# Two products instead of three for small experts, with a branch that only TensorE takes, in a one-core MoE layer

## The chip, the cores and the metric

The kernel runs on one core of a Trainium2 chip. The metric is the device time of one execution in microseconds (us). Five engines work side by side, each with an instruction queue that it executes in order: PE (TensorE, matrix products; PEld is its weight load), DVE (VectorE), ACT (ScalarE), POOL (GpSimd, here mostly indirect DMAs) and SP (which issues the weight loads). They wait for one another through semaphores.

## What is computed

One trunk layer over 1024 tokens of width 1024: a token mixer, and then a hierarchical mixture of experts. The change touches the experts alone. Cut to them, the reference is

```python
g_idx = argmax(hf @ router_w_group + b)            # 1 of 4 groups
top_p, top_i = top_k(softmax(expert logits of that group), 2)
e_idx = g_idx * 8 + top_i                          # 2 of 32 experts for each token
...
hid = silu(x_e @ w_gate[e]) * (x_e @ w_up[e])      # x_e: the tokens of expert e, width 1024; FF = 512
y_e = hid @ w_down[e]                              # back to width 1024
out[token] += weight[token, e] * y_e
```

All in float32. With these inputs the reference's routing gives 21 experts at most 64 tokens, 6 experts 65 to 128, and 5 experts more than 128 (140, 143, 169, 193 and 194).

## The kernel before

The kernel runs the mixer, then the routing, and then a loop over the 32 experts that is fully unrolled in Python (L1823 to L1881), in the order `seq`. An expert's tokens are gathered into blocks of 128 slots (rows that no token fills are padding). The five experts with more than 128 tokens have a second block, called over.

Float32 accuracy comes from splitting both operands of a product in a high and a low part that TensorE multiplies at full rate: `split` (L90) writes high with ACT and low = source - high with DVE, and `mm3` (L94) makes high*high, high*low and low*high. The weights of an expert are six granules of 1 MB, loaded by SP into a ring of eight buffers (`raw`), and `spl(e, i)` splits granule i of expert e in two halves: two ACT instructions (`hi`, 128x1024) and two DVE instructions (`lo`, 128x1024). Granules 0 and 1 are gate and up of the first half of the width, 2 and 3 of the second half, 4 and 5 the down projection.

One iteration of the loop, for expert e, does in the order of the code:

- `part(e, 1, o, ...)` for gate (o = 0) and up (o = 1): the second half of the width, 4 times `mm3` each, 128x512 products that add in the PSUM banks `g` and `u`. Between the two, `xhalf` transposes the first half of the next expert's tokens (4 transposes, then `split` into `xh`, `xl`).
- If expert e has a second block (`tc.If` in L1831), the same for it. All engines take this branch.
- `act`: silu of bank `g` on ACT, times bank `u` on DVE, in `sg`.
- `part(e + 1, 0, 0, ...)`: gate of the next expert's first half. Then `hsplit`: four transposes of `sg`, and `split` into `hh`, `hl`.
- `xhalf` of the next expert's second half, `part(e + 1, 0, 1, ...)`, the branch of L1851 for second blocks, and `down(e, ...)`: 8 times `mm3` into the banks `y`.
- `emit`: two DVE instructions weigh `y` into `yt`, and POOL scatters `yt` to DRAM.

The `spl` calls for the following expert stand between these steps, and their places set the order of the `hi` on ACT and of the `lo` on DVE. Nothing is reordered at run time.

Of the kernel before, what the change touches and what calls it, by code (L numbers as in the profile page):

```python
# [20 lines left out]
P = 128  # L21
T = 1024
# [12 lines left out]
NB = 8  # L35
BIG = 128.0
HUGE = 1e30

# [11 lines left out]
def block_kernel(ctx: ExitStack, tc: tile.TileContext, I, out):  # L50
# [1201 lines left out]
    def pick(pl, i):  # L1252
        rr = sb(pl, "rr", [P, 2, 6, NE], BF16, bufs=3)
        return rr, V.tensor_tensor(rr, k2[:, i].unsqueeze(2).to_broadcast([P, 2, 6, NE]),
                                   vals[:, i].unsqueeze(3).to_broadcast([P, 2, 6, NE]), op=ALU.mult)
# [3 lines left out]
    def place(pl, i, b0, rr, ps):  # L1259
        oa = sb(pl, "oa", [P, 2, 2 * P], BF16, bufs=3)  # L1260
# [16 lines left out]
    def decode(pl, ps, out, ints):  # L1277
        us = []
        for b in range(2):
            v = ps[b].rearrange("p (f e) -> p f e", f=6)  # L1280
            u = sb(pl, f"u{b}", [P, 6, NE], bufs=1) if pl else sb(gt, "sgm", [P, 6, NE])
            us.append(u)
            V.tensor_copy(u[:, 0:2], v[:, 0:2])
            V.scalar_tensor_tensor(u[:, 0], u[:, 1], float(P), u[:, 0], op0=ALU.mult, op1=ALU.add)
            for dst in (out, ints)[::-1] if ints is not None else (out,):
                V.tensor_scalar(dst[:, b, :, 0], u[:, 0], -1.0, None, op0=ALU.add)
            yield
        for b, u in enumerate(us):
# [377 lines left out]
    def piece(e, i, k, n):  # L1666
        z, w = n * k // D, n * k % D
        return tuple(t_[:, w:w + n] for t_ in SP[e, i, z])

    def xhalf(xg, q, nm="x"):  # L1670
        x = q if nm == "x" else 0
        xh, xl = sb(wk, f"{nm}h{x}", [P, 4, P], F32R), sb(wk, f"{nm}l{x}", [P, 4, P], F32R)
# [45 lines left out]
    def over(e, q, banks):  # L1718
        if q == 0:
            warm(banks[0], 1.3)  # L1720
        xs = xhalf(xos[e % 2], q, "o")
        for o in range(2):
            part(e, q, o, xs, banks[o])

    full = xgs[0][:, 0:NB * NE * 3].rearrange("p (b e f) -> p b e f", b=NB, e=NE)

    def more(e, wf, banks, banks2):
# [6 lines left out]

        def tr(src, nm, n):
            o = sb(wk, nm, [P, 4, P])
            pt = sb(psm, "tp", [P, 4, P], bufs=2)
# [5 lines left out]
        for q in range(2):  # L1743
            xt = tr(xos[0], "xf", q)
# [4 lines left out]
        ht = tr(act(banks, "so"), "xf", 0)  # L1749
        for k in range(4):  # L1750
# [4 lines left out]

    NBV = {}

# [8 lines left out]
    def load_nb(e):  # L1766
        return nc.values_load(nbi[0:1, seq[e]:seq[e] + 1] if type(e) is int else e[0:1, :], min_val=0, max_val=NB)

    GU = [[sb(psm, f"{x}{i}", [P, FF]) for x in "gu"] for i in range(2)]
    ybank = [sb(psm, f"y{n}", [P, 512]) for n in range(2)]  # L1770
# [4 lines left out]
    for e in range(1, NX):  # L1775
        G.memset(xgs[e], 0.0)
        gather(xgs[e], e, 0)
    for o in range(2):
        part(0, 0, o, XA, GU[0][o])
    for x in xos:  # L1780
# [17 lines left out]
    def overflow(wf):  # L1798
        tp = [GU[1][0][:, b * 192:(b + 1) * 192] for b in range(2)]
        for b0 in range(2, NB, 2):  # L1800
            for i in range(NT):
                rr, _ = pick(wk, i)
                for _ in place(wk, i, b0, rr, tp):
                    pass
            for _ in decode(wk, tp, full[:, b0:b0 + 2], None):
                pass
# [16 lines left out]
    for e in range(NE):  # L1823
        nxt = e + 1 < NE
        A, B = GU[e % 2], GU[(e + 1) % 2]
        part(e, 1, 0, XB, A[0])
        if nxt:
            XA = xhalf(xgs[(e + 1) % NX], 0)
        part(e, 1, 1, XB, A[1])
        spl(e + 1, 1)  # L1830
        with tc.If(get_nb(e) > 1):  # L1831
            over(e, 1, B)
            sgo = act(B, "so")
        if not nxt:
# [25 lines left out]
        if not nxt:  # L1860
# [156 lines left out]
```

## Time and profile before

| | |
|---|---|
| median of 3 runs (lowest, highest) | 1670.95 us (1669.13, 1671.73) |
| profiled execution: its own time, its span | 1674.46 us, 1672.6 us |
| granted TensorE clock, mean over the span | 0.984 |
| busy: PE, DVE, ACT, POOL | 94%, 79%, 43%, 20% |
| loop over the experts | from about 890 to 1616 us of the span |

The span runs from the first to the last instruction of the profiled execution. Busy shares are averages over stages with different limits, so the loop has to be read by itself.

### The profile page before, as it was taken

The numbers are of one execution on the slowest core, as the hardware profiler recorded it, in microseconds if no ns is written. First come the engines' busy times: TensorE is split into PE (matmuls) and PEld (weight loads), VectorE is DVE, ScalarE is ACT, GpSimd is POOL, SyncE is SP. The second block draws the span as 40 slices with busy tenths as digits, with TensorE's granted clock in tenths as the row PEclk, the third lists the DMA queues.
The fourth block names the chain that finished last, engine by engine and source line by source line (L and its number), as shares of the span: only waits on it lengthen the run. The fifth ranks groups of instructions, "written<-read, shape, count | busy, mean of one in ns | idle before, by whom it ended". The sixth has DMA issues, their size and how long they took to land.

```text
span 1672.6 us, 23420 instructions
## 1 busy us (share of the span) xinstructions
PE 1570.5 (94%) x7602; PEld 1237.4 (74%) x7602; DVE 1320.1 (79%) x2917; ACT 725.3 (43%) x1053; POOL 330.5 (20%) x264
## 2 busy tenths in 40 slices
PE   7899999899998899999988999999999999999984
PEld 3688888778886777788866777777777777777751
DVE  7858883569998568878876786999986999686877
ACT  1533332341213342231122664777764777465622
POOL 1431000002234300003213121221221212120127
PEclk9999999999998999999989999999999999999998
DMA  8425788742314665656524695999995999676872
GB/s 320 163 76 167 230 244 263 239 166 98 100 60 131 167 179 164 202 194 229 184 77 162 251 340 191 348 364 363 362 345 182 361 356 377 259 284 240 290 296 101
DMA packets 141731, 381.61 MB, mean 228 GB/s; under 512 B 17632, under 2 KB 76160, under 8 KB 116992
## 3 DMA queue, kind: packets, MB, share of 16 engines
q1 hardware_dynamic: 130912, 362.80, 62.2%
q0 software_dynamic: 10656, 16.80, 2.7%
q8 instruction: 83, 1.36, 0.3%
q14 instruction: 80, 0.66, 0.1%
HBM read 336.98 MB, written 68.76 MB: 243 GB/s over the span
## 4 chain that ended last, share of the span: by engine, by line
PE 34%; DMA 24%; issue 21%; DVE 17%; POOL 1%; SPq 1%; POOLq 1%; another core or an unknown queue 0%; ACT 0%; DVEq 0%; ACTq 0%
DMA y_d<-yt,tbi 13%; DMA xo<-h_d,tbi 8%; DVE vs L911 4%; DVE sa L908 4%; PE g L95 3%; PE g L97 3%; PE g L96 3%; PE t L97 2%; PE t L95 2%; PE t L96 2%; PE pm L95 1%; DVE vc L911 1%; PE pm L96 1%; PE pm L97 1%; DVE acc L784 1%
## 5 line engine op out<-in xcount | busy, mean ns | idle before, releaser
L92 DVE TENSOR_TENSOR lo<-raw,hi 128x1024 fp32r<-128x1024 f32 x376 | 440.9, 1221 | 31.5 <-ACT hi L91 21.4
L91 ACT ACTIVATE hi<-raw 128x1024 fp32r<-128x1024 f32 x376 | 372.0, 1051 | 34.0 <-PEq L1858 20.8
L95 PE MATMUL g<-hh,wh 128*128 128x512 f32 x448 | 177.1, 395 | 0.0
L96 PE MATMUL g<-hl,wh 128*128 128x512 f32 x448 | 174.7, 390 | 0.0
L97 PE MATMUL g<-hh,wl 128*128 128x512 f32 x448 | 174.6, 390 | 0.0
L1715 POOL DMA_INDIRECT y_d<-yt,tbi x37 | 92.3, 2495 | 382.0 <-DVE yt L1708 300.4
L95 PE MATMUL y<-hi,hh 128*128 128x512 f32 x256 | 103.0, 402 | 6.1 <-PEq L1858 2.1
L92 POOL TENSOR_TENSOR wl<-raw,wh 128x1024 fp32r<-128x1024 f32 x17 | 41.1, 2419 | 330.8 <-ACT wh L91 330.8
L95 PE MATMUL g<-hi,xh 128*128 128x512 f32 x256 | 102.5, 400 | 4.2 <-ACT xh L91 0.3
L95 PE MATMUL u<-hi,xh 128*128 128x512 f32 x256 | 105.8, 413 | 0.0
L97 PE MATMUL g<-hi,xl 128*128 128x512 f32 x256 | 100.6, 393 | 1.1 <-DVE xl L92 1.1
L97 PE MATMUL u<-hi,xl 128*128 128x512 f32 x256 | 100.9, 394 | 0.0
L97 PE MATMUL y<-hi,hl 128*128 128x512 f32 x256 | 100.5, 392 | 0.0
L96 PE MATMUL g<-lo,xh 128*128 128x512 f32 x256 | 100.3, 392 | 0.0
L96 PE MATMUL u<-lo,xh 128*128 128x512 f32 x256 | 99.9, 390 | 0.0
L96 PE MATMUL y<-lo,hh 128*128 128x512 f32 x256 | 99.8, 390 | 0.0
L91 ACT ACTIVATE xh<-tp 128x512 fp32r<-128x512 f32 x64 | 37.5, 588 | 140.7 <-PE tp L1675 140.7
L95 PEld LDWEIGHTS g<-hh,wh 128*128 128x128 f32 x448 | 84.3, 188 | 19.1 <-issue 2.3
L97 PEld LDWEIGHTS g<-hh,wl 128*128 128x128 f32 x448 | 84.2, 188 | 17.9
L96 PEld LDWEIGHTS g<-hl,wh 128*128 128x128 f32 x448 | 84.3, 188 | 16.7
L610 ACT ACTIVATE sg<-g 128x512 f32<-128x512 f32 x32 | 19.2, 599 | 140.1 <-PE g L97 104.8
L1551 POOL DMA_INDIRECT xg<-h_d,tbi x32 | 34.0, 1063 | 213.6 <-PE tp L1675 160.1
(503 smaller groups left out, 3581.6 us busy)
## 6 DMA issues: line engine op xcount, KB each, us to landing
raw<-in_w_exp SPq DMA_DIRECT2D x192, 1024.0 KB
raw<-in_w_r SPq DMA_DIRECT2D x28, 512.0 KB
w<-w_d SPq DMA_DIRECT2D x32, 384.0 KB
raw<-in_w_ada SPq DMA_DIRECT2D x20, 512.0 KB
sig_d<-sg SPq DMA_DIRECT2D x32, 256.0 KB
rp<-r_d SPq DMA_DIRECT2D x64, 128.0 KB
raw<-in_w_ada SPq DMA_DIRECT2D x6, 1024.0 KB
aw<-in_w_ada SPq DMA_DIRECT2D x12, 512.0 KB
```

The source lines that it names most:

```text
L91: S.activation(hi, src, AF.Copy)
L92: (eng or V).tensor_tensor(lo, src, hi.bitcast(F32), op=ALU.subtract)
L95: PE.matmul(ps, a[0], b[0], start=first, stop=False)
L96: PE.matmul(ps, a[0], b[1], start=False, stop=False)
L97: PE.matmul(ps, a[1], b[0], start=False, stop=last)
L610: S.activation(sg, pg, AF.Sigmoid)
L784: V.scalar_tensor_tensor(acc, w[:, k, :], sc[:, k, 0:1], acc, op0=ALU.mult, op1=ALU.add)
L908: V.tensor_tensor(t[d], cur[:, d].unsqueeze(2).to_broadcast([P, 2, 2, NPAIR]), kc[:, d], op=ALU.mult)
L911: V.tensor_tensor(new[:, d], new[:, d], t[d][:, r], op=ALU.add)
L1551: G.indirect_dma_start(out=xg, out_offset=None, in_=h2_d, in_offset=bass.IndirectOffsetOnAxis(ap=tbi[:, b, seq[e], 0:1], axis=0), bounds_c ...
L1715: G.indirect_dma_start(out=y_d, out_offset=bass.IndirectOffsetOnAxis(ap=tbi[:, b, seq[e], 1:2], axis=0), in_=yt, in_offset=None, bounds_ch ...
```

## The change

Each block of at most 64 tokens gets two products in place of three in gate and up. `xhalf` now writes high and low parts interleaved into one tile `xs` of shape 128 x 4 x 128 x 2, so that the first 64 tokens, high and low, are 128 adjacent columns. With those as the stationary operand, a product with the high part of the weights and one with their low part give a bank whose rows 2t and 2t+1 are the high and the low part of token t, and which have to be added. For larger blocks the three products remain, and both variants are in the program: `part` branches with `tc.If` on a count in units of 64 tokens (`nbh`, read by `few_nb` into registers of TensorE alone). No other engine decides anything there.

The sum of the two rows is made in the transposes ahead of the down projection: `copies` copies both banks to SBUF with ACT, and `fold` multiplies each by a 128x128 matrix `fm`, which is the identity for larger blocks, and adds neighbouring rows for small ones. These are eight ordinary float32 products where `hsplit` had four transposes. silu, the product with up and the split come behind them. The matrix is made for each block by one DVE instruction from the constant `both`.

The order of the steps changes too: the transposes of the next expert's first half stand ahead of `part(e, 1, ...)`, the fold of a second block gets a branch of its own (L1887 in the new numbering), and `down(e, ...)` stands ahead of the branch for second blocks.

```diff
     def xhalf(xg, q, nm="x"):
...
-        split(xh, xl, pt)
-        return xh, xl
-
-    def part(e, q, o, xs, ps_):
-        for z in range(4):
-            mm3(ps_, (xs[0][:, z, :], xs[1][:, z, :]), piece(e, 2 * q + o, z, FF), q == 0 and z == 0, q == 1 and z == 3)
-
-    def act(pgu, nm="sg"):
-        sg = sb(wk, nm, [P, FF])
-        S.activation(sg, pgu[0], AF.Silu)
-        V.tensor_mul(sg, sg, pgu[1])
-        return sg
-
-    def hsplit(hf, a="hh", b="hl"):
+        split(xs[:, :, :, 0], xs[:, :, :, 1], pt)
+        return xs
+
+    def part(e, q, os, xs, banks, blk=0):
+        nb = few_nb(e)
+        with tc.If(nb < 2 * blk + 2) as small:
+            for o in os:
+                for z in range(4):
+                    w = piece(e, 2 * q + o, z, FF)
+                    for x in range(2):
+                        PE.matmul(banks[o], xs[:, z, 0:HB].rearrange("p t x -> p (t x)"), w[x], start=(q == 0 and z == 0 and x == 0),
+                                  stop=(q == 1 and z == 3 and x == 1))
+        with small.Else():
+            for o in os:
+                for z in range(4):
+                    mm3(banks[o], (xs[:, z, :, 0], xs[:, z, :, 1]), piece(e, 2 * q + o, z, FF),
+                        q == 0 and z == 0, q == 1 and z == 3)
+
+    def copies(e, pgu, nm="s", blk=0):
+        fm = sb(wk, nm + "m", [P, P])
+        V.scalar_tensor_tensor(fm, both, few[:, blk, seq[e]:seq[e] + 1], ident, op0=ALU.mult, op1=ALU.add)
+        cs = [sb(wk, nm + x, [P, FF]) for x in "gu"]
+        for c, ps_ in zip(cs, pgu):
+            S.activation(c, ps_, AF.Copy)
+        return cs, fm
+
+    def fold(cs, a="hh", b="hl"):
+        (g, u), fm = cs
         a, b = sb(wk, a, [P, 4, P], F32R), sb(wk, b, [P, 4, P], F32R)
-        pt = sb(psm, "tp", [P, 4, P], bufs=2)
-        for k in range(4):
-            PE.transpose(pt[:, k, :], hf[:, k * P:(k + 1) * P], ident)
-        split(a, b, pt)
+        pts = [sb(psm, "tp", [P, 4, P], bufs=2) for _ in range(2)]
+        for src, pt in ((g, pts[0]), (u, pts[1])):
+            for k in range(4):
+                PE.matmul(pt[:, k, :], src[:, k * P:(k + 1) * P], fm, start=True, stop=True)
+        S.activation(g, pts[0].rearrange("p a b -> p (a b)"), AF.Silu)
+        V.tensor_mul(g, g, pts[1].rearrange("p a b -> p (a b)"))
+        split(a, b, g.rearrange("p (a b) -> p a b", a=4))
         return a, b
...
-        part(e, 1, 0, XB, A[0])
         if nxt:
             XA = xhalf(xgs[(e + 1) % NX], 0)
-        part(e, 1, 1, XB, A[1])
+            few_nb(e + 1)
+        part(e, 1, range(2), XB, A)
+        cs = copies(e, A)
         spl(e + 1, 1)
         with tc.If(get_nb(e) > 1):
             over(e, 1, B)
-            sgo = act(B, "so")
+            cso = copies(e, B, "o", 1)
...
-        sg = act(A)
         if nxt:
             spl(e, 4)
-        if nxt:
-            part(e + 1, 0, 0, XA, B[0])
-        hs = hsplit(sg)
+            part(e + 1, 0, (0,), XA, B)
+        hs = fold(cs)
...
         if nxt:
             spl(e, 5)
+            part(e + 1, 0, (1,), XA, B)
+        with tc.If(get_nb(e) > 1):
+            h_ = fold(cso, "oh", "ol")
+        if nxt:
             XB = xhalf(xgs[(e + 1) % NX], 1)
             gather(xgs[(e + 1) % NX], e + 1 + NX, 0)
-            part(e + 1, 0, 1, XA, B[1])
+            down(e, hs, ybank)
         with tc.If((load_pair(e) if nxt else get_nb(e)) > 1):
             with tc.If(get_nb(e) > 1):
-                h_ = hsplit(sgo, "oh0", "ol0")
                 banks = [sb(psm, "tp", [P, 512], bufs=2) for _ in range(2)]
                 down(e, h_, banks)
                 emit(banks, e, 1)
...
-        if nxt:
-            down(e, hs, ybank)
         spl(e + 1, 2)
```

The rest of the diff makes `nbh` and the flags `few` from the counts (four small DVE instructions), makes `both` once (three), and moves scratch tiles of a path for more than 256 tokens in one expert, which these inputs don't take.

How the change moves instructions is seen at two places in the middle of the loop. The first is DVE between the `lo` of granule 4 and that of granule 5 of expert e. Before, the product with up (L1686) and the low part of the hidden layer (`hl`) stood apart:

```order
L1686 TENSOR_TENSOR sg<-sg,u_9275 128x512
L92 TENSOR_TENSOR lo<-raw,hi 128x1024 x2
L92 TENSOR_TENSOR hl<-tp,hh 128x512
L1767 TENSOR_LOAD nbi
L1844 COMPARE_AND_BRANCH
L1844 UNCONDITIONAL_BRANCH x2
L92 TENSOR_TENSOR lo<-raw,hi 128x1024 x2
L92 TENSOR_TENSOR xl_13747<-tp,xh_13746 128x512
```

In the changed kernel the same stretch of DVE's queue reads (L1721 is the product with up, L93 the low part in `split`):

```order
L93 TENSOR_TENSOR lo<-raw,hi 128x1024 x2
L1721 TENSOR_TENSOR sg<-sg,tp 128x512
L93 TENSOR_TENSOR hl<-sg,hh 128x512
L1797 TENSOR_LOAD nbi
L1882 COMPARE_AND_BRANCH
L1882 UNCONDITIONAL_BRANCH x2
L1692 UNCONDITIONAL_BRANCH
L93 TENSOR_TENSOR lo<-raw,hi 128x1024 x2
L1887 COMPARE_AND_BRANCH
```

The two `lo` have moved ahead of the product, and `hl` follows it directly; a branch for the fold of a second block has come in behind the next two `lo`.

The second place is PE behind `part(e, 1, ...)`. Here is the changed kernel from the fold of expert e to the small arm of up of the next expert (L1692 is the branch of `part`, L1697 the two products, L1719 the fold):

```order
L1692 UNCONDITIONAL_BRANCH
L1719 MATMUL tp<-sm,sg 128x128 x4
L1719 MATMUL tp<-sm,su 128x128 x4
L1797 TENSOR_LOAD nbi
L1882 COMPARE_AND_BRANCH
L1882 UNCONDITIONAL_BRANCH x2
L1692 COMPARE_AND_BRANCH
L1697 MATMUL u_9281<-hi,x_14803 128x512
L1697 MATMUL u_9281<-lo,x_14803 128x512
```

Before, four transposes of `sg` stood at this place, and no branch around the products behind them. In the changed kernel the small arm ends in a jump over the 12 products of the large arm (24 in `part(e, 1, ...)`); the large arm is reached by a jump over the small one.

## Rows read from the trace of the kernel before

**Rows 1.** Windows: busy us and instructions by engine, clock, DMA share, GB/s

```profile
1160.00:1200.00 40.00, 39.31 (x180) 31.36 (x181) 37.92 (x40) 30.04 (x35) 7.79 (x4) 1.00 0.99 358
1240.00:1280.00 40.00, 37.00 (x168) 28.94 (x167) 23.39 (x25) 19.71 (x24) 2.77 (x2) 1.00 0.63 229
```

**Rows 2.** Timeline of DVE, one iteration: start, us, instruction, [idle before <-releaser]

```profile
1120.64 0.69 DVE L92 TENSOR_TENSOR xl<-tp,xh 128x512 fp32r<-128x512 f32 x1
1121.52 2.36 DVE L92 TENSOR_TENSOR lo<-raw,hi 128x1024 fp32r<-128x1024 f32 x2 [0.19 <-ACT hi L91]
1124.09 0.69 DVE L1686 TENSOR_TENSOR sg<-sg,u 128x512 f32<-128x512 f32 x1 [0.21 <-ACT hi L91]
1124.70 2.36 DVE L92 TENSOR_TENSOR lo<-raw,hi 128x1024 fp32r<-128x1024 f32 x2
1126.97 0.69 DVE L92 TENSOR_TENSOR hl<-tp,hh 128x512 fp32r<-128x512 f32 x1
1127.97 2.36 DVE L92 TENSOR_TENSOR lo<-raw,hi 128x1024 fp32r<-128x1024 f32 x2 [0.31 <-ACT hi L91]
1130.25 0.68 DVE L92 TENSOR_TENSOR xl<-tp,xh 128x512 fp32r<-128x512 f32 x1
1131.14 4.63 DVE L92 TENSOR_TENSOR lo<-raw,hi 128x1024 fp32r<-128x1024 f32 x4 [0.21 <-DVEq L1851]
1135.69 1.41 DVE L1708 SCALAR_TENSOR_TENSOR yt<-y,tbf,g2b 128x512 f32<-128x512 f32 x2
1137.01 2.35 DVE L92 TENSOR_TENSOR lo<-raw,hi 128x1024 fp32r<-128x1024 f32 x2
1139.28 0.69 DVE L92 TENSOR_TENSOR xl<-tp,xh 128x512 fp32r<-128x512 f32 x1
```

**Rows 3.** Timeline of PE around the branch of L1831 and the transposes

```profile
1122.27 0.40 PE L97 MATMUL u<-hi,xl 128*128 128x512 f32 x1
1122.82 0.47 PE L95 MATMUL g<-hi,xh 128*128 128x512 f32 x1
1123.12 0.40 PE L96 MATMUL g<-lo,xh 128*128 128x512 f32 x1
1123.36 0.40 PE L97 MATMUL g<-hi,xl 128*128 128x512 f32 x1
...
1125.43 0.40 PE L97 MATMUL g<-hi,xl 128*128 128x512 f32 x1
1125.66 0.60 PE L1693 MATMUL tp<-ident,sg 128*128 128x128 f32 x4
1126.10 0.60 PE L1675 MATMUL tp<-ident,xg 128*128 128x128 f32 x4
```

**Rows 4.** Waits, 1060 to 1240 us: total us, times, longest

```profile
PEld g L95 <- ACTq L1831: 5.5, 10, 0.6
```

**Rows 5.** Timeline of PE: float32 products of the router, two records for each product

```profile
767.80 1.87 PE L1496 MATMUL misc<-rw,ht 128*128 128x36 f32 x16
```

**Rows 6.** Timeline of the last expert: ACT to DVE

```profile
1604.59 0.60 ACT L91 ACTIVATE hh<-tp 128x512 fp32r<-128x512 f32 x1 [4.46 <-PE tp L1693]
1605.21 0.69 DVE L92 TENSOR_TENSOR hl<-tp,hh 128x512 fp32r<-128x512 f32 x1 [1.38 <-ACTq L1851]
```

**Rows 7.** Timeline: DVE to ACT; ACT takes the first of the two DVE results

```profile
842.43 1.41 DVE L1423 SCALAR_TENSOR_TENSOR h<-x,mv,sc 128x384 f32<-128x384 f32 x2
843.13 0.62 ACT L1424 ACTIVATE h<-h,rs 128x384 f32<-128x384 f32 x1 [4.82 <-DVE h L1423]
```

**Rows 8.** Groups of DVE by form: busy us, mean ns, idle before

```profile
L784 DVE SCALAR_TENSOR_TENSOR acc<-aw,sc,acc 128x128 f32<-128x128 f32 x84 | 29.6, 352 | 3.0
```

**Rows 9.** Timeline of DVE: the weighing before and behind an expert with a second block

```profile
1228.95 1.40 DVE L1708 SCALAR_TENSOR_TENSOR yt<-y,tbf,g2b 128x512 f32<-128x512 f32 x2
...
1288.69 1.40 DVE L1708 SCALAR_TENSOR_TENSOR yt<-y,tbf,g2b 128x512 f32<-128x512 f32 x2
```

**Rows 10.** Waits, 900 to 1600 us, in second blocks

```profile
PE tp L95 <- DVE xl L92: 6.0, 5, 1.2
```

More of the change, by code (lines that the diff above doesn't have):

```diff
@@ L36 @@
 BIG = 128.0
+HB = 64
 HUGE = 1e30
@@ L1252, in pick @@
     def pick(pl, i):
-        rr = sb(pl, "rr", [P, 2, 6, NE], BF16, bufs=3)
+        rr = sb(pl, "rr", [P, 2, 6, NE], BF16, bufs=3) if pl is q1 else pl
         return rr, V.tensor_tensor(rr, k2[:, i].unsqueeze(2).to_broadcast([P, 2, 6, NE]),
@@ L1259, in place @@
     def place(pl, i, b0, rr, ps):
-        oa = sb(pl, "oa", [P, 2, 2 * P], BF16, bufs=3)
+        oa = sb(pl, "oa", [P, 2, 2 * P], BF16, bufs=3) if pl is q1 else pl
         if b0:
@@ L1280, in decode @@
             v = ps[b].rearrange("p (f e) -> p f e", f=6)
-            u = sb(pl, f"u{b}", [P, 6, NE], bufs=1) if pl else sb(gt, "sgm", [P, 6, NE])
+            u = pl[b] if pl else sb(gt, "sgm", [P, 6, NE])
             us.append(u)
@@ L1637, in block_kernel @@
     V.tensor_reduce(nbm, nbi, axis=AX.X, op=ALU.max)
+    nbh = iotab[:, 0:2 * NE].bitcast(I32)
+    V.tensor_scalar(nbh, pc, HB - 1.0, None, op0=ALU.add)
+    V.tensor_scalar(nbh, nbh, 6, None, op0=ALU.logical_shift_right)
+    few = iotab[:, 2 * NE:6 * NE].bitcast(F32).rearrange("p (b e) -> p b e", b=2)
+    for b in range(2):
+        V.tensor_scalar(few[:, b], pc, float(b * P + HB), None, op0=ALU.is_le)
     by_seq = nbi.rearrange("p (g m) -> p m g", g=4)
@@ L1668, in piece @@
         return tuple(t_[:, w:w + n] for t_ in SP[e, i, z])
+    both = sb(xgp, "both", [P, P])
+    V.memset(both, 0.0)
+    V.tensor_reduce(both[:, 0:HB], ident.rearrange("p (t x) -> p t x", x=2), axis=AX.X, op=ALU.add)
+    V.tensor_sub(both, both, ident)
     def xhalf(xg, q, nm="x"):
-        x = q if nm == "x" else 0
-        xh, xl = sb(wk, f"{nm}h{x}", [P, 4, P], F32R), sb(wk, f"{nm}l{x}", [P, 4, P], F32R)
+        xs = sb(wk, f"{nm}{q if nm == 'x' else 0}", [P, 4, P, 2], F32R)
         pt = sb(psm, "tp", [P, 4, P], bufs=2)
@@ L1721, in over @@
         xs = xhalf(xos[e % 2], q, "o")
-        for o in range(2):
-            part(e, q, o, xs, banks[o])
+        part(e, q, range(2), xs, banks, 1)
     full = xgs[0][:, 0:NB * NE * 3].rearrange("p (b e f) -> p b e f", b=NB, e=NE)
@@ L1733, in more, with tr @@
         gather(xos[0], e, 1)
-        def tr(src, nm, n):
-            o = sb(wk, nm, [P, 4, P])
+        def tr(src, n):
+            o = sb(wk, "ou", [P, FF]).rearrange("p (a b) -> p a b", a=4)
             pt = sb(psm, "tp", [P, 4, P], bufs=2)
@@ L1743, in more @@
         for q in range(2):
-            xt = tr(xos[0], "xf", q)
+            xt = tr(xos[0], q)
             for o in range(2):
@@ L1748, in more @@
                               start=(q == 0 and z == 0), stop=(q == 1 and z == 3))
-        ht = tr(act(banks, "so"), "xf", 0)
+        so = sb(wk, "og", [P, FF])
+        S.activation(so, banks[0], AF.Silu)
+        V.tensor_mul(so, so, banks[1])
+        ht = tr(so, 0)
         for k in range(4):
@@ L1754, in more @@
         emit(banks2, e, 1)
-    NBV = {}
+    NBV, NBH = {}, {}
     def get_nb(e):
@@ L1767, in load_nb, with few_nb @@
         return nc.values_load(nbi[0:1, seq[e]:seq[e] + 1] if type(e) is int else e[0:1, :], min_val=0, max_val=NB)
+    def few_nb(e):
+        if e not in NBH:
+            NBH[e] = nc.values_load(nbh[0:1, seq[e]:seq[e] + 1], engines=[mybir.EngineType.PE], min_val=0, max_val=2 * NB,
+                                    skip_runtime_bounds_check_because="a count of at most T tokens in units of 64")
+        return NBH[e]
     GU = [[sb(psm, f"{x}{i}", [P, FF]) for x in "gu"] for i in range(2)]
@@ L1777, in block_kernel @@
         gather(xgs[e], e, 0)
-    for o in range(2):
-        part(0, 0, o, XA, GU[0][o])
+    part(0, 0, range(2), XA, GU[0])
     for x in xos:
@@ L1799, in overflow @@
         tp = [GU[1][0][:, b * 192:(b + 1) * 192] for b in range(2)]
+        cv = xos[1]
+        u6 = [cv[:, b * 192:(b + 1) * 192].rearrange("p (f e) -> p f e", f=6) for b in range(2)]
+        rr = cv[:, 384:576].bitcast(BF16).rearrange("p (x f e) -> p x f e", x=2, f=6)
+        oa = cv[:, 576:832].bitcast(BF16).rearrange("p (x s) -> p x s", x=2)
         for b0 in range(2, NB, 2):
             for i in range(NT):
-                rr, _ = pick(wk, i)
-                for _ in place(wk, i, b0, rr, tp):
+                pick(rr, i)
+                for _ in place(oa, i, b0, rr, tp):
                     pass
-            for _ in decode(wk, tp, full[:, b0:b0 + 2], None):
+            for _ in decode(u6, tp, full[:, b0:b0 + 2], None):
                 pass
```

## The prediction

> **What bounds the kernel now.** I read the windows of the loop first, then one iteration of DVE and of PE in the timeline. Where no expert has a second block, PE is busy 39.31 of 40 us, DVE 37.92, ACT 30.04, and the DMA engines 0.99 of the time; around a second block DVE falls to 23.39 and DMA to 0.63 while PE stays at 37.00 [rows 1]. So TensorE sets the pace, but nothing else is far behind. An iteration lasts from one `xl` to the next but one: 1139.28 - 1120.64 = 18.64 us [rows 2].
>
> PE's 18.64: 72 products at (1125.43 - 1123.36) / 9 = 0.23 (0.2285 over longer stretches), 16.45; 12 transposes at (1126.10 - 1125.66) / 4 = 0.11, 1.32; and two places with idle time, L1831 and L1851. At L1831 three starts take 1123.12 - 1122.27 = 0.85 where two steps of 0.23 would do: 0.39 lost [rows 3]. That is so in all ten iterations between 1060 and 1240 us, always 0.55 of idle weight load [rows 4], so I take it as the price of a jump over a long body, whatever ACT does. Twice: 0.78. Sum 18.55.
>
> DVE's 18.64 [rows 2]: its work is 12 `lo` at 1.135 from start to start (4.55 for the four at 1131.14), two `xl`, one product and one `hl` at 0.61 each, two `yt` at 0.66: 13.62 + 2.44 + 1.32 = 17.38. The rest is four gaps: 0.19 and 0.21 and 0.31 and 0.21, each 0.08 dearer because two neighbours normally overlap by that: 1.24. DVE thus has at most 1.26 us to give away, and this is what the change has to live on.
>
> **The change, part by part.** Times per iteration; k counts how many of e and e + 1 have more than 64 tokens, as an iteration computes the second half of e and the first of e + 1. In the order of the loop k is 0 in 12 iterations, 1 in 17, 2 in 2; the last iteration has no next expert.
>
> *PE, products.* A small half loses 8 products, 1.83. For k = 0 there remain 32 + 24 = 56, 12.80.
> *PE, fold.* Four transposes go, eight float32 products come. The nearest row has two records for each float32 product, 16 records in 1.87, so 0.23 a product [rows 5]; it streams 36 columns where the fold streams 128, but a record of a 128x128 transpose also takes 0.11 [rows 3], so weight load and stream are about equal and I keep 0.23: 1.84. From below it is the transposes' 0.11, 0.88; from above twice 0.23.
> *PE, jumps.* `part` ends in a jump, or starts with one, three times; with L1871, L1887 and L1893 that makes six instead of two. At 0.39: 2.34. From below the four new ones are free: the branch of L1844, over an empty body, stands between the two groups of transposes and costs nothing [rows 3]. From above 0.55. I take 0.39, since the new bodies are long too.
> PE altogether for k = 0: 12.80 + 0.88 (eight transposes) + 1.84 + 2.34 = 17.86; k = 1: 19.69; k = 2: 21.52.
>
> The Trainium skill ("Advanced Engine Details and Errata", Control Flow Timing) puts a branch-always at about 51 ns and a compare-and-branch at about 108 ns. The 0.39 of this trace is several times that. By the page the four new jumps would be near 0.4 together instead of 1.56; that is the first of the rivals below.
>
> *DVE, the split of the hidden layer.* Here is the term that decides. `hl` now follows the product directly, but it needs `hh`, which ACT makes from that product. ACT starts up to 0.1 after a DVE result (0.70 after the first of two that take 1.41 together) [rows 7]; `hh` takes 0.60 and `hl` starts 0.02 behind it [rows 6]. From the start of the product to that of `hl`: 0.69 + 0.09 + 0.60 + 0.02 = 1.40 in place of 0.61, so 0.79 more. Queued behind `hl` are the `lo` of granule 5, which `down` needs, and so everything. The next `hi` stands behind `hh` on ACT, so the gap of 0.31 + 0.08 ahead of that `lo` remains.
> *DVE, the rest.* The matrix `fm`: 352 ns for such an instruction [rows 8], less the overlap 0.3. The branch L1887 is taken past its body like L1851: 0.21 + 0.08 [rows 2]. The jumps of `part` are over nothing on DVE: free. The gap of 0.27 ahead of the `lo` of granule 1 goes, if ACT is ahead there (next point). DVE: 17.38 + 0.3 + 0.79 + 0.39 + 3 x 0.29 = 19.73.
> *ACT.* The two copies (0.6 each) wait for `part(e, 1)` to end, and `hi` of granules 1 and 4 wait behind them. From the end of `hl`: `down` 5.0, jump and transposes 0.85, 16 products 3.66, copies to 10.8, `hi` to 11.85. DVE then has done 2 + 4 `lo`, `xl`, `yt`, 2 `lo`, `xl` and `fm` since, about 12.5. It is not late, by 0.6. If PE slips by more than that, DVE idles here.
> *DMA.* No byte changes; a longer iteration needs less of it.
>
> An iteration takes the longer of both. k = 0: DVE, 19.7, +1.06. k = 1: both at 19.7; two in-order engines that are equally long wait for one another now and then, for which I estimate 0.3 (one gap of the present kind): 20.0, +1.36. k = 2: 21.52, +2.88. Sum 12 x 1.06 + 17 x 1.36 + 2 x 2.88 = 41.6.
>
> *Second blocks.* One adds 1288.69 - 1228.95 - 2 x 18.64 = 22.5 now [rows 9], with PE setting the pace. Three of them hold at most 64 tokens (12, 15, 41): -16 products 3.66, + fold 1.36 (eight at 0.23 less four at 0.11), + two jumps 0.78, and the split of the hidden layer, for which PE waited 6.0 / 5 = 1.2 [rows 10], is now made ahead: -2.7. The two with 65 and 66: +0.9. Sum -6.
> *Ends.* Seven small DVE instructions ahead of the loop, about 1; the last expert's copies and fold lie open, about 2, less the products saved: +2 together.
>
> Sum: 41.6 - 6 + 2 = +37.6. On the profiled execution 1674.46 becomes 1712; it lies 3.5 above the median of the runs, and against that 1670.95 + 37.6 = 1708.5, call it 1708.
>
> **Rivals.**
> *The new jumps are nearly free* (as L1844 is): PE falls to 16.3, 18.1 and 20.0, DVE's 19.7 remains: 29 x 1.06 + 2 x 1.32 - 10 (second blocks) + 2 = +25, 1696. If `fm` and L1887 are hidden as well, DVE is 19.1 and it is 29 x 0.5 + 2.6 - 10 + 2 = +9, 1680. For it speaks L1844, against it that every long body cost 0.39.
> *Faster: DVE's gaps don't add up.* If the gaps of DVE sum to less than 18.64 - 17.68 = 0.96, small iterations get shorter, since PE at 16.3 to 17.9 allows it. The DMA engines, busy 0.99 at 358 GB/s, then stop it near 18.3. This needs PE's jumps cheap too, for k = 1: 29 x -0.34 + 2 x 1.3 - 10 = -17, 1654. Against it: the chain from product to `hl` alone takes 0.79 of the 0.96.
> *No difference*: gaps of 1.1 or so, gains in second blocks against the iterations with k = 2.
> *Dearer: interleaved operands.* No row shows an operand with a stride of 8 bytes. If DVE's and ACT's instructions that write `xs` take twice as long, DVE gains 1.2 an iteration, +37, 1745; if the weight loads of the large arm do (0.19 to 0.38, over the product's 0.23), a large half costs 24 x 0.15 = 3.6 more, 22 halves, near +79. If ACT's copies come late by 1 us it is +30. For it: DVE has no slack; against it: what the engines read is still one run per partition.
> *It does nothing*: TensorE always takes the large arm. Then all iterations take 21.5: +89 and +5 for second blocks, 1765.
>
> **How the numbers follow.** Forecast (both engines priced as above, 1690 to 1726) 0.61; jumps or DVE's gaps cheaper, 1676 to 1690 and its upper end 1696, 0.14; faster 0.07; no difference 0.05; dearer 0.11; does nothing 0.02. The range 1680 to 1735 reaches down to the rival with the cheap jumps and up to where copies come late or jumps cost 0.55 (k = 1 then 20.9 by PE: 17 x 0.9 = +15). Outside lie the faster and equal cases and most of the dear ones, two in ten. Slower by over 0.2%, about 3.3 us and near what this measurement can tell: 0.88; within 0.05; faster 0.07.
>
> **What the profile after would show.** Right: `hl` starts about 1.4 after L1721 in each iteration, with DVE idle <- ACT `hh`; weighings follow one another at 19.7 to 20 for small experts and above 21 where two large ones meet; PE idles 0.5 at each jump of L1692, more in all than now, and waits on DVE. The fold's eight products take 1.8. Wrong: iterations at or under 18.6 for small experts, no idle time at L1692, or PE busy with three products where the count is small. The prediction falls if DVE finds other work between L1721 and `hl`, which the order doesn't show, or if a gap that I priced at nothing (the jumps of `part` on DVE and ACT) costs 0.2 three times.

## The result and the profile after

The changed kernel takes 1832.35 us (median of 4 runs, 1827.37 to 1832.6) against 1671.34 for the kernel before in the same comparison: ratio 1.0957, 95% interval 1.0934 to 1.098. It is slower, as predicted, but by 161 us and not by 37, far outside the range. The profiled execution has a span of 1830.4 us (before 1672.6) and a mean granted clock of 0.953.

The page of the profile after shows the busy time of each engine and the costliest groups (busy us, mean ns | idle time before them and what ended most of it); the last two lines are the same two groups before the change:

```profile
PE 1593.2 (87%) x7662; PEld 1256.8 (69%) x7662; DVE 1338.5 (73%) x2961; ACT 769.1 (42%) x1126; POOL 308.4 (17%) x264
...
L93 DVE TENSOR_TENSOR lo<-raw,hi 128x1024 fp32r<-128x1024 f32 x376 | 442.8, 1221 | 147.2 <-ACT hi L92 138.8
L92 ACT ACTIVATE hi<-raw 128x1024 fp32r<-128x1024 f32 x376 | 373.4, 1049 | 119.3 <-PEq L1893 39.8
...
L1697 PE MATMUL g<-hi,x 128*128 128x512 f32 x168 | 76.9, 458 | 54.4 <-DVE x L93 37.7
...
L1686 PE MATMUL tp<-ident,xg 128*128 128x128 f32 x256 | 41.3, 285 | 54.5 <-ACTq L1887 40.1
L1697 PEld LDWEIGHTS g<-hi,x 128*128 128x128 f32 x168 | 35.0, 208 | 71.8 <-ACTq L1871 60.9
```

```profile
L92 DVE TENSOR_TENSOR lo<-raw,hi 128x1024 fp32r<-128x1024 f32 x376 | 440.9, 1221 | 31.5 <-ACT hi L91 21.4
L91 ACT ACTIVATE hi<-raw 128x1024 fp32r<-128x1024 f32 x376 | 372.0, 1051 | 34.0 <-PEq L1858 20.8
```

The work has not become dearer: a `lo` still takes 1.2 us and a `hi` 1.05. What has grown is the idle time ahead of them, from 31.5 to 147.2 us and from 34.0 to 119.3. Three of the five names that end idle time after the change have a q: that is the sequencer of another engine at a branch (L1871, L1887, L1893), so an engine waited until another one had passed a branch.

The windows of [rows 1], after:

```profile
1160.00:1200.00 40.00, 29.70 (x139) 23.13 (x137) 31.62 (x35) 27.08 (x33) 4.76 (x3) 0.96 0.82 305
1240.00:1280.00 40.00, 32.92 (x155) 26.20 (x156) 30.94 (x32) 26.02 (x32) 4.37 (x3) 0.96 0.84 312
```

Between 1160 and 1200 us PE was busy 39.31 of 40 and DVE 37.92; now 29.70 and 31.62, and the DMA share has fallen from 0.99 to 0.82. No engine is full any more, and neither are the DMA engines, so the waits have to be read.

One iteration without second block and with two small experts, on DVE (start, us, instruction [idle before <- releaser]):

```profile
1257.18 1.40 DVE L1736 SCALAR_TENSOR_TENSOR yt<-y,tbf,g2b 128x512 f32<-128x512 f32 x2
...
1267.17 0.69 DVE L1721 TENSOR_TENSOR sg<-sg,tp 128x512 f32<-128x512 f32 x1 [0.61 <-PE tp L1719]
1268.56 0.69 DVE L93 TENSOR_TENSOR hl<-sg,hh 128x512 fp32r<-128x512 f32 x1 [0.70 <-ACT hh L92]
...
1277.91 2.36 DVE L93 TENSOR_TENSOR lo<-raw,hi 128x1024 fp32r<-128x1024 f32 x2 [2.49 <-ACT hi L92]
1280.19 1.40 DVE L1736 SCALAR_TENSOR_TENSOR yt<-y,tbf,g2b 128x512 f32<-128x512 f32 x2
```

From one weighing to the next 1280.19 - 1257.18 = 23.01 us; before 18.64 [rows 2]. `hl` stands 1268.56 - 1267.17 = 1.39 behind the product: the term that was to decide is there (1.40 predicted), but a gap of 2.49 behind ACT weighs more. The same iteration on ACT and on PE:

```profile
1258.59 0.60 ACT L1710 ACTIVATE su<-u 128x512 f32<-128x512 f32 x1
1259.07 2.01 ACT L92 ACTIVATE hi<-raw 128x1024 fp32r<-128x1024 f32 x2
1261.25 2.01 ACT L92 ACTIVATE hi<-raw 128x1024 fp32r<-128x1024 f32 x2 [0.17 <-ACTq L1871]
...
1268.43 1.99 ACT L92 ACTIVATE hi<-raw 128x1024 fp32r<-128x1024 f32 x2
...
1276.82 3.90 ACT L92 ACTIVATE hi<-raw 128x1024 fp32r<-128x1024 f32 x4 [2.84 <-PEq L1893]
```

```profile
1258.02 0.40 PE L1697 MATMUL u<-lo,x 128*128 128x512 f32 x1
1261.60 0.47 PE L1697 MATMUL g<-hi,x 128*128 128x512 f32 x1 [3.18 <-DVE x L93]
...
1264.11 0.63 PE L1697 MATMUL g<-lo,x 128*128 128x512 f32 x1
1264.54 1.64 PE L1719 MATMUL tp<-sm,sg 128*128 128x128 f32 x8
...
1268.52 0.40 PE L1697 MATMUL u<-lo,x 128*128 128x512 f32 x1
1270.52 0.66 PE L1686 MATMUL tp<-ident,xg 128*128 128x128 f32 x4 [1.60 <-ACTq L1887]
...
1276.30 0.39 PE L98 MATMUL y<-hi,hl 128*128 128x512 f32 x1
```

Read in a ring: ACT's `hi` at 1276.82 waits 2.84 until PE has passed L1893, which in the new order stands behind the 24 products of `down` (the last starts at 1276.30). DVE's `lo`, and behind them in its queue the `x` (the low part of the next tokens) that PE's next gate products need, come late by that. PE waits 3.18 for such an `x`, then 1.60 at L1887 for ACT, which gets there only behind silu, `hh` and two `hi` (to 1270.42). So `down` is late, and with it PE at L1893.

The waits between 1140 and 1290 us (who waited <- for whom: total us, times, longest):

```profile
DVE lo L93 <- ACT hi L92: 21.0, 20, 3.9
PEld g L1697 <- ACTq L1871: 20.0, 6, 3.6
...
ACT hi L92 <- PEq L1893: 12.7, 4, 4.2
PEld tp L1686 <- ACTq L1887: 12.5, 6, 2.9
```

Behind the idle time the clock falls (windows: busy us by engine, then clock, DMA share, GB/s):

```profile
1256.00:1262.00 6.00, 2.82 (x13) 2.04 (x12) 6.00 (x9) 5.83 (x8) 1.72 (x1) 1.00 0.68 253
1262.00:1266.40 4.40, 4.40 (x20) 3.82 (x19) 4.19 (x4) 1.39 (x3) 0.00 (x0) 0.61 0.82 290
```

Behind the 3.18 us in which PE stood, the granted clock is 0.61 for 4.4 us: products start 0.43 apart (1264.54 - 1264.11) where they start 0.23 apart at full speed, near the ratio of the levels 1.2 and 2.4 GHz. PE's iteration adds up: 56 products and 8 transposes 13.7 and the fold 1.7 at full speed, 5.6 in three gaps (3.35, 1.77 and 0.46 beyond the normal step), 1.6 for the clock, and five steps that are 0.1 longer than normal: 23.1. What the clock is worth to the whole iteration is another question, which the last section takes up.

### The profile page after: what moved, and what is told of

Its sections match the earlier page's. It is cut to its first block, busy times and chain, and to the rows that moved or that the text cites. A ratio compares the mean times of both kernels' runs of the same rounds, so it can differ in the third digit from the quotient of the medians.

```text
span 1830.4 us, 24156 instructions
## 1 busy us (share of the span) xinstructions
PE 1593.2 (87%) x7662; PEld 1256.8 (69%) x7662; DVE 1338.5 (73%) x2961; ACT 769.1 (42%) x1126; POOL 308.4 (17%) x264
## 3 DMA queue, kind: packets, MB, share of 16 engines
q8 instruction: 108, 1.77, 0.4%
## 5 line engine op out<-in xcount | busy, mean ns | idle before, releaser
L93 DVE TENSOR_TENSOR lo<-raw,hi 128x1024 fp32r<-128x1024 f32 x376 | 442.8, 1221 | 147.2 <-ACT hi L92 138.8
L92 ACT ACTIVATE hi<-raw 128x1024 fp32r<-128x1024 f32 x376 | 373.4, 1049 | 119.3 <-PEq L1893 39.8
L1743 POOL DMA_INDIRECT y_d<-yt,tbi x37 | 65.9, 1780 | 399.0 <-DVE yt L1736 300.3
L1697 PE MATMUL g<-hi,x 128*128 128x512 f32 x168 | 76.9, 458 | 54.4 <-DVE x L93 37.7
L96 PE MATMUL y<-hi,hh 128*128 128x512 f32 x256 | 108.1, 422 | 5.1 <-ACTq L1887 5.1
L1552 POOL DMA_INDIRECT xg<-h_d,tbi x32 | 40.4, 1264 | 381.8 <-PE tp L1686 314.7
L93 POOL TENSOR_TENSOR wl<-raw,wh 128x1024 fp32r<-128x1024 f32 x17 | 41.0, 2409 | 329.4 <-ACT wh L92 329.4
L1686 PE MATMUL tp<-ident,xg 128*128 128x128 f32 x256 | 41.3, 285 | 54.5 <-ACTq L1887 40.1
L1697 PEld LDWEIGHTS g<-hi,x 128*128 128x128 f32 x168 | 35.0, 208 | 71.8 <-ACTq L1871 60.9
L1686 PEld LDWEIGHTS tp<-ident,xg 128*128 128x128 f32 x256 | 27.4, 141 | 77.8 <-ACTq L1887 51.2
L1697 PE MATMUL g<-lo,x 128*128 128x512 f32 x168 | 74.1, 441 | 1.6 <-DVE lo L93 1.6
L912 DVE TENSOR_TENSOR vs<-vs,sa 128x32 f32<-128x32 f32 x512 | 75.2, 201 | 0.0
L1697 PE MATMUL u<-hi,x 128*128 128x512 f32 x168 | 67.7, 403 | 0.0
```

The source lines that it names most:

```text
L92: S.activation(hi, src, AF.Copy)
L93: (eng or V).tensor_tensor(lo, src, hi.bitcast(F32), op=ALU.subtract)
L96: PE.matmul(ps, a[0], b[0], start=first, stop=False)
L912: V.tensor_tensor(new[:, d], new[:, d], t[d][:, r], op=ALU.add)
L1552: G.indirect_dma_start(out=xg, out_offset=None, in_=h2_d, in_offset=bass.IndirectOffsetOnAxis(ap=tbi[:, b, seq[e], 0:1], axis=0), bounds_c ...
L1697: PE.matmul(banks[o], xs[:, z, 0:HB].rearrange("p t x -> p (t x)"), w[x], start=(q == 0 and z == 0 and x == 0), stop=(q == 1 and z == 3 an ...
```

## The experiments

The letters in the expectations: W is the theory that engines wait for one another at the branches that all of them take; J that the jumps themselves, TensorE's own with them, are the price; L that ACT is late at L1871 because its two copies stand ahead of granule 1 and of the branch. Four edits undo or move one part of the change each. Ratios are to the kernel before, which ran beside each group of runs with medians from 1669.43 to 1673.68 us; so differences of a few us between runs of different groups mean little. A small iteration is one in which both experts have at most 64 tokens.

```diff
# D: down back behind the branch for second blocks
-            down(e, hs, ybank)
         with tc.If((load_pair(e) if nxt else get_nb(e)) > 1):
...
+        if nxt:
+            down(e, hs, ybank)
         spl(e + 1, 2)
# F: the fold of a second block back in the body, no branch L1887
-        with tc.If(get_nb(e) > 1):
-            h_ = fold(cso, "oh", "ol")
...
             with tc.If(get_nb(e) > 1):
+                h_ = fold(cso, "oh", "ol")
# H: hh and hl between the halves of granule 5 (hs = fold(cs, later=nxt))
-            spl(e, 5)
+            spl(e, 5, (0,))
+            hs = hs()
+            spl(e, 5, (1,))
# S: the split of granule 1 ahead of the copies
-        cs = copies(e, A)
         spl(e + 1, 1)
+        cs = copies(e, A)
```

**a1_down_back: D alone.**

> The changed kernel, with down(e) back behind the branch for second blocks (L1893). Theory W (two new waits, made by where the branches stand): ACT's hi of granule 3 reuses a buffer that the branch's body may still read, so it waits until PE has passed L1893, which now stands behind the 24 products of down; with down back, ACT's idle time there (2.8 us in an iteration of 23.0) goes, and an iteration of small experts falls to about 20.5 us, the kernel to about 1760. Rival J (the new jumps, the longer fold and the chain through the hidden layer are simply dear, wherever down stands): iterations stay at 22.5 to 23, the kernel within 15 us of 1832.

Measured 1831.07 us, ratio 1.0953 (1.086 to 1.1046): no change, a miss. Most small iterations fell from 23.0 to about 21.3, but iterations with a large expert rose as often as they fell, and second blocks became longer: PE now waits at L1871 (23.5 us in all between 1100 and 1300 us, 10.6 in the changed kernel).

**a2_fold_back: F alone.**

> The changed kernel, with the fold of a second block back inside the branch of L1894, so that the branch L1887 is gone. Theory W: PE's transposes of the next tokens' second half no longer wait until ACT, behind silu, hh and two hi, has passed L1887 (1.6 to 2.5 us of idle PE in an iteration); an iteration of small experts falls from 23.0 to about 21.4 us, the kernel to about 1785. Rival J: it saves one jump, 0.4 us an iteration, and the kernel comes to about 1820.

Measured 1801.84, ratio 1.0778 (1.0699 to 1.0858): 30 us back, half way between the two expectations.

**a3_both_back: D and F.**

> Both undone: down behind the branch for second blocks, the fold of a second block inside it. Theory W: both waits go; what is left is what the prediction priced, DVE with the chain from the product to hl, about 19.4 us an iteration without L1887, the kernel between 1700 and 1735. Rival J: iterations above 21.5 us, the kernel above 1800.

Measured 1806.04, ratio 1.0804 (1.0717 to 1.089): no better than F alone. My first theory, that the two places explain the loss, fell. What was left is seen on PE:

```profile
1226.40 0.39 PE L98 MATMUL u<-hi,x 128*128 128x512 f32 x1
1229.41 0.51 PE L1697 MATMUL g<-hi,x 128*128 128x512 f32 x1 [2.62 <-ACTq L1871]
```

At that time ACT makes its second copy at 1226.83 and then two `hi` to 1229.31, and only then passes L1871. This is the place of L1831 of before, where the wait was 0.55 [rows 4].

**a4_hl_apart: D, F and H.**

> As a3_both_back, and the split of the hidden layer moved behind the first half of granule 5, so that one hi on ACT and one lo on DVE stand between the product with up and hh, hl. If DVE sets the pace in a3_both_back and its gap of 0.8 us ahead of hl counts in full: 0.5 to 0.8 us less an iteration, 15 to 25 us less than a3_both_back. If the bound there is the chain from PE through hl to down: no less, or up to 15 us more, since hl comes later.

Measured 1793.98, ratio 1.0731 (1.0655 to 1.0808): 12 us less than a3, between the two expectations and within the uncertainty of the two runs.

**b1_split_ahead: S alone.**

> The changed kernel with one edit: the split of granule 1 (two hi on ACT, two lo on DVE) stands ahead of the two copies instead of behind them. Theory L (read from the traces of the runs so far): PE's products behind the branch L1871 write a bank that the branch's body reads on ACT, so PE waits until ACT has passed L1871, and ACT gets there only behind the copies (which wait for the end of part(e, 1)) and the two hi; with the hi ahead, PE's wait there falls from about 2.6 us to under 1. Alone, with the waits at L1887 and L1893 still there, I expect 20 to 40 us less than 1832: 1792 to 1812. Rival J (the price of the jumps and of the longer work on PE): within 8 us of 1832, and PE's wait shows up elsewhere.

Measured 1796.61, ratio 1.0744 (1.0711 to 1.0776): as L expected. 36 us came from two lines of code exchanged, with the same instructions. In this run small iterations and those with a large expert take the same 22.3 us wherever the clock stays at full speed, so here PE's own products don't set the pace.

**b2_all_four: D, F, H and S.**

> a4_hl_apart (down and the second block's fold back, hl apart) with the split of granule 1 ahead of the copies as well. Theory L: no engine waits for another to pass a branch for longer than before the change; iterations of small experts fall from 20.4 to 18.7 to 19.3, where DVE's own work is the bound, and the kernel from 1794 to 1735 to 1755. Rival J: PE's own 17.9 to 18.5 with its jumps and the dependent chain through the fold hold it at 20, above 1780.

Measured 1702.32, ratio 1.018 (1.0142 to 1.0217), better than expected. D alone gives 0, F 30, S 36, and D, F and H together 38, but all four 130. That fits waits that stand in a ring, where the longest that is left sets the pace; no run shows this rule by itself.

**c1, c2, c3: b2 with one edit taken out** (D, F and H).

> b2_all_four (1702 us) with one of its four edits taken out: down stands ahead of the branch L1893 again, as in the changed kernel. Theory W: hi of granule 3 on ACT reuses a buffer that this branch's body may read, so ACT waits for PE to pass it, now behind 24 more products; ACT comes some 2.8 us later with granule 3, and DVE with it: 1 to 2.3 us an iteration, 1735 to 1770. Rival (a1_down_back changed the kernel's time by nothing): within 10 us of 1702.

> b2_all_four with the fold of a second block in a branch of its own again (L1887). Theory W: PE's transposes of the next tokens wait until ACT has passed that branch, behind silu, hh and two hi: 1 us later, and one jump of 0.4 us: 0.7 to 1.4 us an iteration; second blocks gain 1 to 2 us each by the earlier fold: 1720 to 1740. Rival J (only the jump counts): 1705 to 1715.

> b2_all_four with hh and hl directly behind the product with up again. DVE is then idle for 0.7 us between L1721 and hl. If DVE sets the pace of small iterations (18.2 us in b2_all_four): 0.5 to 0.8 us more in these, 10 to 20 us in all, 1712 to 1722. If PE's chain sets it: no difference or some us less.

Measured 1783.18 (1.0682, 1.0643 to 1.0721), 1704.56 (1.0211, 1.0181 to 1.0242) and 1732.97 (1.0382, 1.0351 to 1.0412). From b2, `down` ahead of the branch costs 81 us, more than I expected; the fold's own branch 2, which is within the uncertainty; `hl` behind the product 31, more; and without S (a4) it is 92. The 2 us of c2 are a balance: its fastest small iterations take 18.77 where those of b2 take 18.21, with PE waiting at the fold's branch for up to 0.9, and its second blocks with the two iterations around them are 0.7 to 2.3 shorter. The waits of c1, 1100 to 1300 us, in which only `down` stands as in the changed kernel (L1895 is its branch for second blocks, L1873 the earlier one):

```profile
DVE lo L93 <- ACT hi L92: 22.2, 12, 2.5
ACT hi L92 <- PEq L1895: 21.2, 7, 3.3
PEld g L1697 <- ACTq L1873: 16.8, 6, 3.5
```

ACT waits for PE at the later branch, so it is late at the next earlier one, where PE waits for it. c3 has DVE's iteration as I predicted it, but for the branch L1887, with DVE idle for no more than 0.70 at a time, at branches and behind ACT:

```profile
1113.69 1.40 DVE L1736 SCALAR_TENSOR_TENSOR yt<-y,tbf,g2b 128x512 f32<-128x512 f32 x2
...
1124.60 0.69 DVE L93 TENSOR_TENSOR hl<-sg,hh 128x512 fp32r<-128x512 f32 x1 [0.70 <-ACT hh L92]
...
1133.28 1.40 DVE L1736 SCALAR_TENSOR_TENSOR yt<-y,tbf,g2b 128x512 f32<-128x512 f32 x2
...
1152.63 1.40 DVE L1736 SCALAR_TENSOR_TENSOR yt<-y,tbf,g2b 128x512 f32<-128x512 f32 x2
```

The first of these two iterations has one large half and takes 19.59 us, the second is small and takes 19.35; the sum for DVE without L1887 is 19.73 - 0.29 = 19.44.

**b3_always_two and b4_always_three: b2 without TensorE's branch**, with always two or always three products. b3 leaves out the tokens of a block beyond the 64th.

```diff
# b3 in part; b4 keeps the mm3 loop instead, and its few is never true
-        with tc.If(nb < 2 * blk + 2) as small:
-            for o in os:
...
+        for o in os:
+            for z in range(4):
```

> b2_all_four without TensorE's branch: always the two products, also for blocks of more than 64 tokens, whose tokens beyond the 64th are left out. No jump of L1692, 56 products in every iteration. Theory L: with the waits at the branches gone DVE is the bound for small experts, so these gain at most 0.5 us; the 19 iterations with a large expert fall to the same length: 20 to 40 us below b2_all_four. Rival J: three jumps and their serial cost are worth 1.2 us or more in every iteration, 45 to 70 us below b2_all_four.

> b2_all_four without TensorE's branch: always the three products, with the fold by the identity. 72 products, no jump of L1692. Theory L: PE is then the bound at 16.45 + 0.88 + 1.84 + 0.78 = 19.95 and its waits, about 20.5 us in every iteration: the kernel between 1730 and 1765, near b2_all_four, so that the saved products are worth no more than the jumps cost. Rival: the saved products count in full (3.66 an iteration of small experts, 21 halves of 31), and it is 40 to 80 us slower than b2_all_four.

Measured 1667.38 (0.9973, 0.9946 to 1.0) and 1762.52 (1.054, 1.0493 to 1.0587). b4 has 20.6 to 20.9 an iteration without a second block, b3 18.2 everywhere, b2 18.2 where both experts are small. So the products that the branch saves are worth 60 us against b4; my expectation that they are not felt missed. b3 is 35 us below b2, as L expected. But even with two products for everything, b3 is hardly below the kernel before. One of its iterations as a window:

```profile
1092.51:1110.73 18.22, 16.23 (x82) 12.94 (x81) 17.79 (x20) 15.04 (x19) 3.92 (x2) 1.00 0.99 376
```

DVE is busy 17.79 of 18.22, and its only idle time is two gaps of 0.21 at its own branches, so DVE sets 18.2. The DMA engines are as full, at 0.99, but none of these gaps ends with a transfer. That is about the most that this design can give in this order of steps.

The price of TensorE's branch can be read from b2 itself, an iteration with the large arm at full clock:

```profile
1165.76 0.40 PE L1697 MATMUL u<-lo,x 128*128 128x512 f32 x1
1166.89 0.51 PE L96 MATMUL g<-hi,x 128*128 128x512 f32 x1 [0.73 <-ACTq L1873]
...
1169.57 0.39 PE L98 MATMUL g<-hi,x 128*128 128x512 f32 x1
1169.81 1.05 PE L1719 MATMUL tp<-sm,sg 128*128 128x128 f32 x8
1170.69 1.06 PE L1719 MATMUL tp<-sm,su 128*128 128x128 f32 x8
1171.51 0.49 PE L96 MATMUL u<-hi,x 128*128 128x512 f32 x1
...
1174.17 0.39 PE L98 MATMUL u<-hi,x 128*128 128x512 f32 x1
1174.40 0.60 PE L1686 MATMUL tp<-ident,xg 128*128 128x128 f32 x4
```

From the last gate product to the fold 0.24, from the last up product to the transposes 0.23, which is the step of a product: `part`'s branches cost PE 0.00 to 0.02 here, and behind the small arm of up, whose jump goes over 12 products, it is the same in all 17 such iterations of d1 between 1040 and 1600 us. The jump over 24 products at the end of `part(e, 1, ...)` doesn't show either: where PE waits for nothing but the branch behind it, d1's next gate starts 1.12 to 1.13 behind the last up product, after the small arm, which ends in that jump, and after the large one, which doesn't. The branch that all engines take, one row up, costs 1166.89 - 1165.76 - 0.23 = 0.90. The fold's eight products take 1171.51 - 1169.81 = 1.70.

**d1_second_three: b2, second blocks as before** (three products, silu, product with up and four transposes, no copies and no fold).

> b2_all_four, but second blocks take three products without TensorE's branch, and silu, product and four transposes as before the change, without copies and fold. Theory: of the five second blocks, each 2.6 us dearer in b2_all_four than before the change, the lost fold, jumps and open chain through the hidden layer give back more than the 16 products (3.7 us) that three of them save: 5 to 15 us less than 1702. Rival: the products count in full, 5 to 10 us more.

Measured 1682.46, ratio 1.0079 (1.0048 to 1.011): 20 us better than b2, more than I expected.

**d2_copies_behind, d3_matrix_ahead, e1_copies_behind.** Is that 0.90 the jump or the wait, and is it the rest of the loss? d2 is d1 with the copies behind the branch, d3 also makes `fm` ahead of the transposes, e1 does d2's edit on the changed kernel.

```diff
-        cs = copies(e, A)
         with tc.If(get_nb(e) > 1):
...
+        cs = copies(e, A)
```

> d1_second_three with the two copies behind the branch for second blocks in place of ahead of it: one edit. Waiting (PE's first product of the next expert stands 0.90 behind the last one because ACT passes the branch only behind its copies): 0.90 falls to the 0.3 to 0.4 that the branch L1851 of before shows, which the 19 iterations with at least one large expert feel, 19 x 0.5 = 10 us: 1668 to 1676. The rival, that 0.90 is the jump over the long body: it stays 0.90 and the time 1679 to 1685.

> d2_copies_behind with the matrix fm made at the start of the iteration in place of with the copies. If the fold of small experts, which starts 0.6 late behind DVE, is felt: 2 to 6 us less than d2_copies_behind. The rival, that DVE itself sets these iterations at 18.2 and only the order of its work changes: within 2 us of d2_copies_behind.

> The changed kernel with its two copies behind the branch L1871 in place of ahead of it: one edit. Waiting: ACT reaches the branch with its two hi of granule 1 as before, but no longer behind the end of part(e, 1), so PE's 2.6 to 3.6 us at L1871 go; down and the fold's branch stay where they are and keep their waits, so the time is near that of b1_split_ahead: 1785 to 1805. The rival, that the wait is PE's own jump: 1825 to 1840.

Measured 1682.15 (1.0075, 1.005 to 1.0099), 1680.52 (1.006, 1.0037 to 1.0083) and 1800.13 (1.077, 1.0738 to 1.0803). e1 came as expected: with ACT earlier at the branch, 32 us come back on the changed kernel. In d2 the place shows

```profile
1160.18 0.40 PE L1697 MATMUL u<-lo,x 128*128 128x512 f32 x1
1161.08 0.51 PE L96 MATMUL g<-hi,x 128*128 128x512 f32 x1 [0.51 <-PEq L1875]
```

1161.08 - 1160.18 - 0.23 = 0.67, and now PE's own sequencer is named: of 0.90 about 0.25 was ACT, and about 0.65 remains when ACT has passed earlier (its first copy behind the branch starts at 1159.81). Neither theory had it whole, and the time did not move: the fold waits 0.3 to 0.8 for `fm` instead, and d3, which takes that away, stays within the uncertainty of d2.

Where d3 is still slower is not the middle of the loop. Its weighings of the first expert, of the last expert but one that has a second block, and of the last expert, and behind them the last of the kernel before:

```profile
947.69 1.40 DVE L1741 SCALAR_TENSOR_TENSOR yt<-y,tbf,g2b 128x512 f32<-128x512 f32 x2
...
1480.61 1.41 DVE L1741 SCALAR_TENSOR_TENSOR yt<-y,tbf,g2b 128x512 f32<-128x512 f32 x2
...
1622.74 1.40 DVE L1741 SCALAR_TENSOR_TENSOR yt<-y,tbf,g2b 128x512 f32<-128x512 f32 x2
```

```profile
1614.14 0.74 DVE L1708 SCALAR_TENSOR_TENSOR yt<-y,tbf,g2b 128x512 f32<-128x512 f32 x1
1616.11 0.75 DVE L1708 SCALAR_TENSOR_TENSOR yt<-y,tbf,g2b 128x512 f32<-128x512 f32 x1 [1.23 <-issue]
```

The first two stand at 944.20 and 1479.79 in the kernel before. So d3 gains 535.6 - 532.9 = 2.7 us in the middle, and loses 3.5 ahead of it. A weighing is two instructions; the second of d3's last one starts at 1623.40, 142.8 behind 1480.61, and before at 1616.11, 136.3 behind 1479.79: 6.5 lost at the end. No version with the branch beats the kernel before, and with so small a gain in the middle, and b3 so little below 1, none of these orders promises to.

## Why the prediction was wrong

The direction was right; the size was wrong by 124 us, most of it because the forecast left out the time in which PE and ACT wait for one another at branches. Point by point:

- **What bounds the kernel**: right. PE full, DVE close behind it, and DVE the one that has to live with the change.
- **The product and `hl`**: right. 1.39 for 1.40; taken alone (c3 against b2) it costs 31 us, 1.0 an iteration for 0.79.
- **The iteration by DVE**, 19.7: right for a loop without the waits (19.35 in c3, which lacks the 0.29 of L1887). Without that chain DVE comes to 18.2 and not to 18.64, since the gaps behind ACT go as well; that was the ground of the rival *faster*.
- **The fold**: 1.70 for 1.84. **The products saved**: worth 60 us from b4 to b2, where PE would set the pace otherwise.
- **The jumps**: wrong. Each of the four new ones was priced at 0.39, from L1831, "whatever ACT does". TensorE's own branches cost 0.00 to 0.02. L1831 was no row for them: there all engines branch. Such a branch costs PE 0.39 in the kernel before (0.32 to the first start, as the others are counted here), 0.65 to 0.90 and 2.6 to 3 in other orders of the same instructions, so ACT matters. The rival with nearly free jumps was right in this. The Trainium skill's 51 and 108 ns ("Advanced Engine Details and Errata", Control Flow Timing) are more than these rows show behind TensorE's own branches; the rows decide.
- **ACT**: this is the step that failed. "It is not late, by 0.6" counted only what ACT needs to do for DVE, by durations. It left out that ACT's `hi` wait for PE to pass L1893 (2.84, up to 4.2), and that PE waits for ACT to pass L1871 (2.6 to 3.6) and L1887 (1.6 to 2.5). The sum priced each engine by itself and took the longer one; L1887 was priced as a jump (0.39 on PE, 0.29 on DVE) and not as a wait, the new place of `down` at nothing. The *dearer* rival had the copies "late by 1 us" at +30; they were late by more, and not alone.
- **Second blocks**: -6 predicted, or 1.2 less for each. Between 999.87 and 1067.72 us a second block and two iterations take 67.9 against 59.8 before; the three later ones take 69.2, 70.8 and 71.4 against 59.7 to 59.8. With iterations of 23.5, an estimate from those around (22.3 to 24.8), that is 20.9 to 24.4 for the block by itself, against 22.5 before: little or nothing gained, and most of the loss lies in the iterations around it. With the waits gone, d1 is 20 us better than b2 with second blocks as they were, so there the change did not pay.
- **Ends**: +2 predicted; in d3 they cost 3.5 ahead of the first weighing, and 4.0 between the last two experts' weighings (1623.40 - 1600.32 against 1616.11 - 1596.99).
- **The range**, 1680 to 1735, holds c3 at its upper end: 1733, 62 us above the kernel before and not 37.6. c3 is nearest to the kernel that I had priced, with the chain ahead of `hl`, without the long waits, and without the fold's own branch. So 99 of the 161 us go with D, F and S, the three edits that take the long waits away. The other 24 beyond the forecast have another source; second blocks priced too cheap are among them. That b2, at 1702, lies so near 1708 is luck: it lacks the chain of 0.79 that the forecast counted.

That these are waits for another engine to pass a branch is shown by b1, e1 and c1, which move only the place of ACT's or PE's work before a branch and are worth 32 to 81 us. Why an engine waits there is argued from the code, not shown: the body of each of these branches, when it runs, uses a buffer (bank B at L1871, a `tp` bank at L1887, the granule of the next expert's gate at L1893) that the waiting instruction is about to write, and whether the body is skipped is known only when the other engine has passed.

## What to carry to other kernels

A branch that all engines take is a meeting place, even when its body is skipped: before moving work across one, list for each engine what stands ahead of the branch, and price the wait of the engine that next writes a buffer which the body reads (this last part is argued above, not shown). A branch on one engine alone, over that engine's own instructions, cost nothing measurable here. In a loop with several such waits, undo them together before judging one: alone they gave 0, 30 and 36 us, with H 130.

## What was not expected of the hardware

- TensorE's clock falls behind some of these waits: 0.61 granted for 4.4 us behind 3.18 us without products, with products 0.43 apart instead of 0.23. Not every such gap brings a fall, as behind 3.13 us at 1284.61 products start 0.23 apart. PE's own work grows by 1.6 us, but an iteration by less. b1 has two small iterations side by side, one at full clock and one with a fall:

```profile
1244.83:1267.13 22.30, 16.61 (x82) 12.80 (x81) 18.15 (x20) 15.05 (x19) 3.05 (x2) 1.00 0.86 312
1267.13:1290.14 23.01, 17.91 (x82) 14.04 (x81) 18.25 (x21) 15.12 (x19) 4.05 (x3) 0.93 0.82 290
```

  PE is busy 1.3 us longer and the iteration takes 0.7 more; the rest goes into time that PE would have waited. So in this run the clock behind the waits is the smaller part of what they cost.
- A jump over the body of a branch that all engines take left 0.65 us on PE in d2, where ACT had passed, and a jump over 12 or 24 products none. Whether the length of the body makes the difference, or the other engines that branch with it, was not separated.
